# Expert layer of a two-block transformer: 224 tokens gather their rows, 288 meet every expert, value rows inside the planned order

## The chip, the cores and the metric

The kernel runs on one core of one Trainium2 chip. Its engines are PE (matmul; PEld is its weight load), DVE, ACT, POOL and SP, which here only issues DMAs. Sixteen DMA engines move data between DRAM and the on-chip buffer. The metric is device time in microseconds (us), the median of several executions.

## The reference, cut to what matters

The program is a whole network of two blocks on 512 tokens of width 1024. The change lies in its expert layer, the last step of the first block. The layer has 16,384 experts, each a row u and a row v of 1024 numbers. Each token has 8 heads; each head scores two sets of 128 keys, takes the best 16 of each, forms the 256 sums and keeps the best 16. So every token chooses 128 experts:

```python
def peer_ffn(xn, w_query, sub_keys, expert_u, expert_v):
    q = (xn @ w_query).reshape(bsz, seq, PEER_HEADS, 2, PEER_HALF)
    scores = jnp.einsum("bshpd,hpnd->bshpn", q, sub_keys)
    s_top, i_top = lax.top_k(scores, PEER_TOPK)
    ...
    best, pos = lax.top_k(cand, PEER_TOPK)
    idx = jnp.take_along_axis(cand_idx, pos, axis=-1)
    gates = jax.nn.softmax(best, axis=-1)
    ...
        u = expert_u[it]
        v = expert_v[it]
        act = gelu(jnp.einsum("td,ted->te", xt, u))
        return jnp.einsum("te,ted->td", gt * act, v)
```

## The kernel before

The layer is `peer()`. It treats the 512 tokens as four tiles of 128 and in two ways.

**Tokens 0 to 255 (tiles 0 and 1) gather.** `fetch` issues on POOL, for tile `tt` and choice `s`, one indirect DMA that brings to each of 128 partitions (one token each) that token's row of 4 KB: 128 gathers of 512 KB for each tile and each of the two tables `er` (U) and `ev` (V), 512 in all. The rows land in a ring of 8 places that lies in the tiles `xh` and `xl`. A U row is multiplied and summed with the token's vector on DVE (`product`, recorded at L1000, the line of the helper through which the planned part issues DVE work); a V row is scaled and added to `y` on DVE (L1336).

**Tokens 256 to 511 (tiles 2 and 3) meet all experts.** Experts are seen as 128 groups ("U rows" and "V rows" in what follows) of 128. `weights` (L1014) loads one group of 512 KB on SP into one of three tiles `wraw`, `whi`, `wlo` with several buffers each. `hidden` multiplies U row r with the 256 tokens: 8 matmuls of 128x256 (L1063, two instructions each); ACT takes the gelu (L1068) and writes it to DRAM as `ge_d`, except for the last `KEEP` rows, which stay on the chip. `spread` makes for each token a grid of 128 x 128 gates: DVE and ACT build one-hot factors (`sq`, `acc`), a "put" multiplies them (4 matmuls of 128 columns, L1252), ACT copies the result to `gs` (L1255), and after every fourth put SP writes 1 MB of it to `G` in DRAM. V rows need G and ge: DVE multiplies `a = ge * gt` (L1317), PE adds `a` times the V row into `yb` in PSUM (8 matmuls of 128x256, L1339).

**The order.** `first` writes the order of DVE, ACT, POOL and PE by hand with a planner that counts an estimated DVE time. A step is one U row; a step lasts by plan `ROW` = 4.5 us, or 5.3 where a put stands in it. Into each step the planner puts a piece of the selection (`select`, DVE) and row products, one after `PACE` = 2.6 us of planned time while selection lasts and 1.4 after it. POOL fetches up to `LEAD` = 6 rows ahead of the product. Tile 1's choices are selected last, so its rows can be fetched only when selection is over. `second` then opens new pools and goes through V rows 127 to 0: `a` six steps ahead, two gathered V rows for each step, the 8 matmuls. Its DVE order is the program's, the rest is a scheduler's. SP's order is a scheduler's throughout. After the last V row come 4 additions of `yb` to `h`, 16 transposes of `y`, 4 additions of those (L1351), and the next norm's sums.

Of the kernel before, what the change touches and what calls it, by code (L numbers as in the profile page):

```python
# [18 lines left out]
T = 512  # L19
D = 1024  # L20
# [116 lines left out]
NT = T // 2  # L137
RING = 8
LEAD = 6
KEEP = 20  # L140
PACE = (2.6, 1.4)
ROW = (4.5, 5.3)
GATE = 6
# [9 lines left out]
class Build:  # L153
# [810 lines left out]
    def peer(self):  # L964
        tc = self.tc
        with tc.tile_pool(name="pg", bufs=1) as pg:
            self.pg = pg
            self.G = self.dp.tile([16, 128, 16, 8, 16], F32, name="G")
            self.ge_d = [self.dp.tile([128, NT], F32, name=f"ge_d{j}") for j in range(128 - KEEP)]
# [7 lines left out]
            self.xb = pg.tile([128, 8, NT], F32, name="xb")  # L977
# [45 lines left out]
    def fetch(self, upto):  # L1023

        while self.nr < upto:
            table, n = divmod(self.nr, 256)
            tt, s = divmod(n, 128)
            self.nc.gpsimd.indirect_dma_start(  # L1028
                out=self.row(self.nr), out_offset=None,
                in_=self.A[("er", "ev")[table]].rearrange("j p a b -> (j p) (a b)"),  # L1030
                in_offset=bass.IndirectOffsetOnAxis(ap=self.ix[:, tt, s:s + 1], axis=0))
            self.nr += 1

    def product(self, pace):
# [22 lines left out]
    def hidden(self, r):  # L1057
# [4 lines left out]
        for k in range(8):  # L1062
            nc.tensor.matmul(ps[:, :NT], w[:, k], self.xb[:, k], start=k == 0, stop=k == 7)  # L1063

        def done():
            if r < 128 - KEEP:
                ge = self.pg.tile([128, NT], F32, name="ge", bufs=3)
                nc.scalar.activation(ge, ps[:, :NT], AF.Gelu)  # L1068
                nc.scalar.dma_start(self.ge_d[r], ge)
            else:  # L1070
                ge = self.ge[r] = self.pg.tile([128, NT], F32, name=f"ge{r}")
                nc.scalar.activation(ge, ps[:, :NT], AF.Gelu)
        self.later(1, done)

    def first(self, pt, pw, pps):
# [908 lines left out]
```

## Time and profile before

| | us |
|---|---|
| median of three executions (2762.29 to 2764.92) | 2762.43 |
| the profiled execution | 2763.71 |
| its span, first to last instruction | 2761.9 |
| expert layer, U rows begin to V rows end, about 618 to 1834 | 1216 |

The profile is one execution; times below are microseconds from the start of its span. A row that groups instructions gives their busy time, the mean of one in ns, and how long the engine had been idle just before them, with what ended that idleness. A row of a timeline gives start, length, engine, line, operation and operands, and in brackets the idle time before. Engine busy shares are averages over stages of different kinds, so stretches are read one by one.

### The profile page before, as it was taken

The numbers are of one execution on the slowest core, as the hardware profiler recorded it, in microseconds if no ns is written. First come the engines' busy times: TensorE is split into PE (matmuls) and PEld (weight loads), VectorE is DVE, ScalarE is ACT, GpSimd is POOL, SyncE is SP. The second block draws the span as 40 slices with busy tenths as digits, with TensorE's granted clock in tenths as the row PEclk, the third lists the DMA queues.
The fourth block names the chain that finished last, engine by engine and source line by source line (L and its number), as shares of the span: only waits on it lengthen the run. The fifth ranks groups of instructions, "written<-read, shape, count | busy, mean of one in ns | idle before, by whom it ended". The sixth has DMA issues, their size and how long they took to land.

```text
span 2761.9 us, 33459 instructions
## 1 busy us (share of the span) xinstructions
PE 2446.6 (89%) x11548; PEld 2020.4 (73%) x11548; DVE 1829.5 (66%) x3670; ACT 933.1 (34%) x1806; POOL 1318.7 (48%) x930
## 2 busy tenths in 40 slices
PE   7999998999889997784988888888999998999997
PEld 5778877878778886663866766776777786777776
DVE  6654353357999997657666666676697757666226
ACT  4432343331147775400000000022477734333323
POOL 5433357343333256646554445654324555455543
PEclk9999999999999999897999999999999999999998
DMA  5311123139999999999999999972202252222332
GB/s 193 100 61 31 47 75 125 49 126 340 330 311 339 333 344 410 407 410 407 407 405 405 405 405 405 402 267 66 81 24 74 94 161 81 92 84 92 105 115 86
DMA packets 227882, 600.26 MB, mean 217 GB/s; under 512 B 25601, under 2 KB 90753, under 8 KB 225281
## 3 DMA queue, kind: packets, MB, share of 16 engines
q1 hardware_dynamic: 126688, 298.75, 31.3%
q0 software_dynamic: 73728, 268.47, 25.1%
q10 hardware_dynamic: 27296, 30.90, 3.2%
q8 instruction: 92, 1.51, 0.2%
q14 instruction: 78, 0.63, 0.1%
HBM read 556.09 MB, written 41.94 MB: 217 GB/s over the span
## 4 chain that ended last, share of the span: by engine, by line
PE 31%; DVE 27%; DMA 23%; issue 8%; ACT 6%; POOL 4%; ACTq 0%; SPq 0%; DVEq 0%; POOLq 0%
PE mm L224 7%; PE mm L225 7%; PE mm L223 6%; DMA gl<-ge_d 6%; DVE y L1868 5%; DMA G<-gs 5%; DMA wraw<-in_ev_dram 3%; DMA xl<-in_ev_dram,ix 3%; PE mm L1063 3%; DMA whi<-in_ev_dram 2%; DVE xl L1000 2%; DVE xh L1000 2%; ACT whi L216 2%; PE dl L737 2%; DMA gt<-G 1%
## 5 line engine op out<-in xcount | busy, mean ns | idle before, releaser
L219 POOL TENSOR_TENSOR wlo<-wraw,whi 128x1024 fp32r<-128x1024 f32 (+5 forms) x212 | 466.2, 2205 | 467.0 <-ACT whi L216 461.1
L216 ACT ACTIVATE whi<-wraw 128x1024 fp32r<-128x1024 f32 (+4 forms) x213 | 204.2, 965 | 830.3 <-DMA wraw<-in_w_in_dram 567.4
L225 PE MATMUL mm<-xh,wlo 128*128 128x512 f32 (+1 forms) x1016 | 408.1, 402 | 20.5 <-POOL wlo L219 20.5
L224 PE MATMUL mm<-xl,whi 128*128 128x512 f32 (+1 forms) x1016 | 408.5, 403 | 3.3 <-DVE xl L338 2.3
L223 PE MATMUL mm<-xh,whi 128*128 128x512 f32 (+1 forms) x1016 | 404.9, 401 | 6.4 <-ACT xh L335 3.0
L225 PEld LDWEIGHTS mm<-xh,wlo 128*128 128x128 f32 (+1 forms) x1016 | 193.5, 190 | 68.8 <-POOL wlo L219 32.5
L1028 POOL DMA_INDIRECT xh<-in_ev_dram,ix x128 | 167.6, 1310 | 159.4 <-DVE y L1336 141.7
L1028 POOL DMA_INDIRECT xh<-in_er_dram,ix x128 | 145.1, 1133 | 194.3 <-DVE xh L1000 56.5
L1028 POOL DMA_INDIRECT xl<-in_er_dram,ix x128 | 148.9, 1163 | 172.1 <-DVE xl L1000 49.3
L1339 PE MATMUL yb<-a,wlo 128*128 128x256 f32 x688 | 169.4, 403 | 67.4 <-issue 40.7
L224 PEld LDWEIGHTS mm<-xl,whi 128*128 128x128 f32 (+1 forms) x1016 | 193.8, 191 | 45.9 <-DVE xl L338 6.1
L223 PEld LDWEIGHTS mm<-xh,whi 128*128 128x128 f32 (+1 forms) x1016 | 193.0, 190 | 46.3 <-ACT xh L335 3.9
L1336 DVE SCALAR_TENSOR_TENSOR y<-xl,gate,y 128x1024 f32<-128x1024 f32 x128 | 164.5, 1285 | 71.9 <-DMA xl<-in_ev_dram,ix 69.9
L1339 PEld LDWEIGHTS yb<-a,wlo 128*128 128x128 f32 x688 | 137.3, 203 | 96.2 <-issue 69.1
L1336 DVE SCALAR_TENSOR_TENSOR y<-xh,gate,y 128x1024 f32<-128x1024 f32 x126 | 163.5, 1298 | 41.5 <-DMA xh<-in_ev_dram,ix 40.3
L1868 DVE SCALAR_TENSOR_TENSOR y<-u,cvec,y 128x511 f32<-128x511 f32 (+1 forms) x88 | 137.0, 1560 | 74.6 <-ACT y L1866 73.2
L1339 PE MATMUL yb<-a,wraw 128*128 128x256 f32 x688 | 163.8, 393 | 21.7 <-DMA wraw<-in_ev_dram 20.7
L1028 POOL DMA_INDIRECT xl<-in_ev_dram,ix x128 | 132.8, 1037 | 104.5 <-DVE y L1336 81.2
L1000 DVE SCALAR_TENSOR_TENSOR xh<-xh,xt 128x1024 f32<-128x1024 f32 x128 | 155.8, 1217 | 38.1 <-DMA xh<-in_er_dram,ix 37.4
L1339 PE MATMUL yb<-a,whi 128*128 128x256 f32 x672 | 160.2, 393 | 22.5 <-DMA whi<-in_ev_dram 22.4
L1063 PE MATMUL mm<-xb,wlo 128*128 128x256 f32 x672 | 161.3, 396 | 16.7 <-DMA wlo<-in_eu_dram 9.9
L1000 DVE SCALAR_TENSOR_TENSOR xl<-xl,xt 128x1024 f32<-128x1024 f32 x128 | 155.9, 1218 | 28.3 <-DMA xl<-in_er_dram,ix 27.9
(654 smaller groups left out, 5108.7 us busy)
## 6 DMA issues: line engine op xcount, KB each, us to landing
wraw<-in_w_in_dram SPq DMA_DIRECT2D x57, 512.0 KB, 3.5
wraw<-in_w_up_dram SPq DMA_DIRECT2D x44, 512.0 KB, 3.5
wraw<-in_eu_dram SPq DMA_DIRECT2D x43, 512.0 KB, 6.6
whi<-in_eu_dram SPq DMA_DIRECT2D x43, 512.0 KB, 6.7
wlo<-in_ev_dram SPq DMA_DIRECT2D x43, 512.0 KB, 16.8
wraw<-in_ev_dram SPq DMA_DIRECT2D x43, 512.0 KB, 16.8
wlo<-in_eu_dram SPq DMA_DIRECT2D x42, 512.0 KB, 7.4
whi<-in_ev_dram SPq DMA_DIRECT2D x42, 512.0 KB, 16.8
```

Source lines behind the costliest of these rows:

```text
L216: nc.scalar.activation(hi, src, AF.Copy)
L219: (eng_lo or nc.vector).tensor_tensor(lo, src, hi.bitcast(F32), op=OP.subtract)
L223: t.matmul(ps, wh, xh, start=first, stop=False)
L224: t.matmul(ps, wh, xl, start=False, stop=False)
L225: t.matmul(ps, wl, xh, start=False, stop=last)
L737: te.matmul(ps[:, h * 128:(h + 1) * 128], lhs(h), rhs(h), start=True, stop=True)
L1000: return getattr(self.nc.vector, name)(out, *a, **kw)
L1028: self.nc.gpsimd.indirect_dma_start(out=self.row(self.nr), out_offset=None, in_=self.A[("er", "ev")[table]].rearrange("j p a b -> (j p) (a ...
L1063: nc.tensor.matmul(ps[:, :NT], w[:, k], self.xb[:, k], start=k == 0, stop=k == 7)
L1336: keep(v.scalar_tensor_tensor(y, r, a, y, op0=OP.mult, op1=OP.add))
L1339: te.matmul(yb[d // 2][:, d % 2], w[:, d], a, start=n == 0 and d % 2 == 0, stop=n == 127, skip_group_check=True)
L1868: v.scalar_tensor_tensor(y[:, j:], u[:, :T - j], w(2 - j), y[:, j:], op0=OP.mult, op1=OP.add)
```

## The change

`NT`, the number of tokens that gather, goes from 256 to 224. Tile 1 is split: its first 96 tokens gather, its last 32 join tiles 2 and 3, so that ND = 288 tokens meet all experts. Gathers of tile 1 bring rows to 96 partitions, and the products on them work on 96 partitions. U and V matmuls, gelus and gate products have 288 columns in place of 256, `ge_d` tiles are 128x288, and `G` has 18 blocks of 16 tokens in place of 16 (72 puts in place of 64). `KEEP` is 14 in place of 20. One-hot factors are made on ACT for the fourth part of every second block only, in place of every block.

`first` and `second` become one function, `experts`, with one planned loop of 256 steps: 128 U rows, then 128 V rows in the order 119 to 112, 127 to 120, 111 to 0. Four small functions serve the V steps: `ahead` (weights and ge, five steps ahead, in the U loop's last steps already), `gates` (eight rows of G at a time into one half of a tile that holds `q` until then), `gated` (the product of ge and gates, three steps ahead, into one of 7 slices of a `gs` buffer) and `value` (8 matmuls of 128x288 into 8 banks of PSUM that bear the names `sp`, `gp`, `mm`). The two sums `y` lie in the places of `kz` and `eq`. The planner goes on placing products of gathered V rows through all 256 steps. `ROW` becomes 4.4, 4.8 (with a put) and 3.7 (V step). After the loop come 8 additions of 128x288, 16 transposes, 4 additions of 128x2x224, and then the norm's sums.

```diff
-                self.first(pt, pw, pps)
+                self.experts(pt, pw, pps)
             self.np_open()
-            with tc.tile_pool(name="pv", bufs=2) as pv, \
-                    tc.tile_pool(name="pps", bufs=1, space=PSUM) as pps:
-                self.second(pv, pps)
+            for d in range(8):
+                self.stat2(d)
+                self.raw(d, self.gp[:, d:d + 1])
...
-NT = T // 2
+NT = 224
+ND = T - NT
+NB = ND // 16
+TOK = (128, NT - 128, 0, 0)
 RING = 8
 LEAD = 6
-KEEP = 20
+KEEP = 14
 PACE = (2.6, 1.4)
-ROW = (4.5, 5.3)
-GATE = 6
+ROW = (4.4, 4.8, 3.7)
+AOFF = 24
...
+            m = TOK[tt]
             self.nc.gpsimd.indirect_dma_start(
-                out=self.row(self.nr), out_offset=None,
+                out=self.row(self.nr)[:m], out_offset=None,
                 in_=self.A[("er", "ev")[table]].rearrange("j p a b -> (j p) (a b)"),
-                in_offset=bass.IndirectOffsetOnAxis(ap=self.ix[:, tt, s:s + 1], axis=0))
+                in_offset=bass.IndirectOffsetOnAxis(ap=self.ix[:m, tt, s:s + 1], axis=0))
...
+        table, n = divmod(n, 256)
         tt, s = divmod(n, 128)
-        r = self.row(n)
+        m = TOK[tt]
+        r = self.row(self.nf)[:m]
         self.nf += 1
-        self.dve("scalar_tensor_tensor", r, r, 1.0, self.xt[:, tt], op0=OP.mult, op1=OP.mult,
-                 accum_out=self.hid[:, tt, s:s + 1])
+        if table == 0:
+            self.dve("scalar_tensor_tensor", r, r, 1.0, self.xt[:m, tt], op0=OP.mult,
+                     op1=OP.mult, accum_out=self.hid[:m, tt, s:s + 1])
+        else:
+            a, y = self.gate[:m, tt, s:s + 1], self.y[tt][:m]
+            if s == 0:
+                self.dve("tensor_scalar", y, r, a, None, op0=OP.mult)
+            else:
+                self.dve("scalar_tensor_tensor", y, r, a, y, op0=OP.mult, op1=OP.add)
...
-            nc.tensor.matmul(ps[:, :NT], w[:, k], self.xb[:, k], start=k == 0, stop=k == 7)
+            nc.tensor.matmul(ps[:, :ND], w[:, k], self.xb[:, k], start=k == 0, stop=k == 7)
         def done():
             if r < 128 - KEEP:
-                ge = self.pg.tile([128, NT], F32, name="ge", bufs=3)
-                nc.scalar.activation(ge, ps[:, :NT], AF.Gelu)
+                ge = self.pg.tile([128, ND], F32, name="ge", bufs=5)
...
-                self.known = 128 * tt + (h0 + n) * K
+                self.known = 128 * tt + (h0 + n) * K if tt == 0 else 512
...
-            for tb in range(8):
+            for tb in range((128 - TOK[tt]) // 16):
...
-                        if t4 == 3:
+                        if t4 == 3 and tb % 2:
...
+        grids = (x for tt in (2, 3, 1) for x in spread(tt))
         load = lambda r: self.wts.update({r: self.weights(A["eu"][r])}) if r < 128 else None
+        yb, gt, vw, va = [], {}, {}, {}
+        order_v = [*range(119, 111, -1), *range(127, 119, -1), *range(111, -1, -1)]
+        def ahead(i):
+            if not 0 <= i < 128:
+                return
+            j = order_v[i]
+            vw[j] = self.weights(A["ev"][j])
+            if j < 128 - KEEP:
+                self.ge[j] = self.pg.tile([128, ND], F32, name="ge", bufs=5)
+                nc.sync.dma_start(self.ge[j], self.ge_d[j])
+        def gates(i):
+            if i % 8 or not 0 <= i < 128:
+                return
+            if not gt:
+                self.gt2 = pt.tile([128, 2, NB * 128], F32, name="q")
+                self.y = [pt.tile([128, D], F32, name="kz"), pw.tile([128, D], F32, name="eq")]
+                self.a = pw.tile([128, 2048], F32, name="gs", bufs=2)
+            gt[i // 8] = self.gt2[:, i // 8 % 2].rearrange("p (b j t) -> p b j t", j=8, t=16)
+            nc.sync.dma_start(gt[i // 8], self.G[order_v[i] // 8])
+        def gated(i):
+            if not 0 <= i < 128:
+                return
+            j = order_v[i]
+            c = AOFF + i % 7 * ND
+            va[j] = self.a[:, c:c + ND]
+            v("tensor_tensor", va[j].rearrange("p (b t) -> p b t", t=16),
+              self.ge.pop(j).rearrange("p (b t) -> p b t", t=16), gt[i // 8][:, :, j % 8],
+              op=OP.mult)
+        def value(i):
+            j = order_v[i]
+            if not yb:
+                yb.extend([pps.tile([128, T], F32, name="sp", bufs=2) for _ in range(2)] +
+                          [pps.tile([128, T], F32, name="gp", bufs=3) for _ in range(3)] +
+                          [self.pp.tile([128, T], F32, name="mm") for _ in range(3)])
+            a, w = va.pop(j), vw.pop(j)
+            for d in range(8):
+                te.matmul(yb[d][:, :ND], w[:, d], a, start=i == 0, stop=i == 127)
...
-            while self.step < 128 or work or grids or self.after or self.nf < 256:
+            while self.step < 256:
+                i = self.step - 128
                 self.due(False)
                 load(self.step + 5)
-                if self.step < 128:
+                ahead(i + 5)
+                gates(0 if i == -6 else i + 11 if i > -6 else -1)
+                gated(i + 3)
+                if i < 0:
                     self.hidden(self.step)
-                end += ROW[(self.step, True) in self.after]
+                    end += ROW[(self.step, True) in self.after]
+                else:
+                    value(i)
+                    end += ROW[2]
...
-                        self.spent = end if self.nf == 256 else min(end, self.when + PACE[1])
+                        self.spent = end if self.nf == 512 else min(end, self.when + PACE[1])
...
-    def second(self, pv, pps):
...
+                assert i != -7 or not grids
+            self.when = -99.0
+            while self.product(0.0):
+                self.when = -99.0
         self.xh, self.xl = (self.cp.tile([128, 8, T], F32R, name=n) for n in ("xh", "xl"))
-        for b in range(4):
+        for d in range(8):
+            h = self.h[:, d, NT:]
+            v("tensor_tensor", h, h, yb[d][:, :ND], op=OP.add)
+        for d in range(0, 8, 2):
             tp = self.pp.tile([128, T], F32, name="mm").rearrange("p (e t) -> p e t", e=2)
             for e in range(2):
                 for tt in range(2):
-                    d = 2 * b + e
-                    te.transpose(tp[:, e, tt * 128:(tt + 1) * 128],
-                                 self.y[:, tt, d * 128:(d + 1) * 128], self.ident)
-            for t, o in ((yb[b], NT), (tp, 0)):
-                h = self.h[:, 2 * b:2 * b + 2, o:o + NT]
-                nc.vector.tensor_tensor(h, h, t, op=OP.add)
-            for d in (2 * b, 2 * b + 1):
-                self.stat2(d)
-                self.raw(d, self.gp[:, d:d + 1])
+                    m = TOK[tt]
+                    te.transpose(tp[:, e, tt * 128:tt * 128 + m],
+                                 self.y[tt][:m, (d + e) * 128:(d + e + 1) * 128],
+                                 self.ident[:m, :m])
+            h = self.h[:, d:d + 2, :NT]
+            v("tensor_tensor", h, h, tp[:, :, :NT], op=OP.add)
```

**SP, where U rows end and V rows begin.** `eu` and `ev` are the U and V weights, `G` is the grid in DRAM, `gt` (before) and `q` (after) are its copies on the chip, `gl` is a ge that is read back; the numbers behind names count tiles. Before:

```order
L1014 DMA wraw_9139<-in_ev_dram 128x1024
L1014 DMA whi_9157<-in_ev_dram 128x1024
L1311 DMA gt_9095<-G_4299 128x2048
L1311 DMA gt_9153<-G_4299 128x2048
L1311 DMA gt_9283<-G_4299 128x2048
L1315 DMA gl_9349<-ge_d107_4407 128x256
L1315 DMA gl_9367<-ge_d106_4406 128x256
L1315 DMA gl_9385<-ge_d105_4405 128x256
L1315 DMA gl_9403<-ge_d104_4404 128x256
L1014 DMA wlo_9173<-in_ev_dram 128x1024
L1311 DMA gt_9421<-G_4299 128x2048
```

After, from the last write of the grid on:

```order
L1019 DMA wlo_8999<-in_eu_dram 128x1024
L1273 DMA G_4299<-gs_8780 128x16x128
L1019 DMA wraw_9018<-in_eu_dram 128x1024
L1307 DMA q_9039<-G_4299 128x2304
L1019 DMA whi_9037<-in_eu_dram 128x1024
L1307 DMA q_9039<-G_4299 128x2304
L1019 DMA wlo_9063<-in_ev_dram 128x1024
L1019 DMA wraw_9082<-in_ev_dram 128x1024
L1019 DMA whi_9101<-in_ev_dram 128x1024
```

Before, three readings of G stand behind the last U weight and nine V weights. Now the first reading stands among the last U weights, two rows behind the last write of G, and the V weights follow behind the readings.

**DVE, in the middle of the V rows.** `a` (before) and `gs` (after) receive ge times gates, `y` (before) and `kz` (after) are tile 0's sum, and `xh`, `xl` are the ring of gathered rows. Before:

```order
L1336 SCALAR_TENSOR_TENSOR y_9090<-xl_4697,gate_4411,y_9090 128x1024
L1317 TENSOR_TENSOR a_9643<-gl_9641,gt_9567 128x256
L1336 SCALAR_TENSOR_TENSOR y_9090<-xh_4696,gate_4411,y_9090 128x1024
L1336 SCALAR_TENSOR_TENSOR y_9090<-xl_4697,gate_4411,y_9090 128x1024
L1317 TENSOR_TENSOR a_9661<-gl_9659,gt_9567 128x256
```

After:

```order
L1005 TENSOR_TENSOR gs_9042<-ge_9835,q_9039 128x288
L1005 SCALAR_TENSOR_TENSOR kz_9040<-xh_4702,gate_4418,kz_9040 128x1024
L1005 SCALAR_TENSOR_TENSOR kz_9040<-xl_4703,gate_4418,kz_9040 128x1024
L1005 TENSOR_TENSOR gs_9042<-ge_9854,q_9039 128x288
L1005 SCALAR_TENSOR_TENSOR kz_9040<-xh_4702,gate_4418,kz_9040 128x1024
L1005 SCALAR_TENSOR_TENSOR kz_9040<-xl_4703,gate_4418,kz_9040 128x1024
L1005 SCALAR_TENSOR_TENSOR kz_9040<-xh_4702,gate_4418,kz_9040 128x1024
L1005 TENSOR_TENSOR gs_9042<-ge_9871,q_9039 128x288
```

Two row products stand between two gate products before; two or three do now.

**DVE, at the end of the layer.** `h` is the layer's result, `yb` (before) and `sp` (after) are matmul sums, `eq` is tile 1's sum. Before:

```order
L1336 SCALAR_TENSOR_TENSOR y_9090<-xl_4697,gate_4411,y_9090 128x1024
L1336 SCALAR_TENSOR_TENSOR y_9090<-xh_4696,gate_4411,y_9090 128x1024
L1336 SCALAR_TENSOR_TENSOR y_9090<-xl_4697,gate_4411,y_9090 128x1024
L1351 TENSOR_TENSOR h_69<-h_69,yb0_9091 128x2x256
L1351 TENSOR_TENSOR h_69<-h_69,yb1_9092 128x2x256
```

After:

```order
L1005 SCALAR_TENSOR_TENSOR eq_9041<-xh_4702,gate_4418,eq_9041 96x1024
L1005 SCALAR_TENSOR_TENSOR eq_9041<-xl_4703,gate_4418,eq_9041 96x1024
L1005 TENSOR_TENSOR gs_9042<-ge_11301,q_9039 128x288
L1005 TENSOR_TENSOR gs_9042<-ge_11317,q_9039 128x288
L1005 TENSOR_TENSOR gs_9042<-ge_11332,q_9039 128x288
L1005 TENSOR_TENSOR h_69<-h_69,sp_9163 128x288
L1005 TENSOR_TENSOR h_69<-h_69,sp_9164 128x288
```

The last gathered row stood right ahead of the additions; now three gate products stand between them, and so three V rows' matmuls come after the last gathered row.

## Rows read from the trace of the kernel before

**Rows 1.** The page: the span, and GB/s moved in each of its 40 equal slices.

```profile
span 2761.9 us, 33459 instructions
...
GB/s 193 100 61 31 47 75 125 49 126 340 330 311 339 333 344 410 407 410 407 407 405 405 405 405 405 402 267 66 81 24 74 94 161 81 92 84 92 105 115 86
```

**Rows 2.** Stretches: length, then busy PE, PEld, DVE, ACT, POOL, PEclk, DMA share, GB/s.

```profile
618.00:800.00 182.00, 160.35 (x716) 137.95 (x715) 160.82 (x515) 31.32 (x67) 66.81 (x61) 0.97 0.93 329
800.00:1011.00 211.00, 197.34 (x1052) 175.00 (x1051) 204.63 (x671) 157.06 (x370) 68.89 (x62) 0.98 0.97 333
1011.00:1240.00 229.00, 181.64 (x858) 155.85 (x856) 160.51 (x305) 93.32 (x228) 142.73 (x119) 0.92 1.03 402
1240.00:1280.00 40.00, 0.00 (x0) 0.00 (x0) 27.65 (x46) 0.58 (x2) 23.25 (x23) 0.56 1.03 411
1280.00:1834.00 554.00, 482.85 (x2048) 401.63 (x2049) 367.57 (x381) 1.06 (x1) 295.56 (x249) 0.94 1.03 403
```

**Rows 3.** DMA traffic from 618 to 1011, and its total and queues from 1280 to 1834.

```profile
DMA packets 62379, 130.10 MB, mean 331 GB/s; under 512 B 4794, under 2 KB 35898, under 8 KB 62347
...
DMA packets 70860, 223.42 MB, mean 403 GB/s; under 512 B 7883, under 2 KB 21707, under 8 KB 68965
## 3 DMA queue, kind: packets, MB, share of 16 engines
q0 software_dynamic: 35893, 130.67, 59.6%
q1 hardware_dynamic: 34938, 92.37, 42.7%
```

**Rows 4.** Groups by line, 600 to 1860: busy, mean ns, idle before.

```profile
L1339 PE MATMUL yb<-a,wlo 128*128 128x256 f32 x688 | 169.4, 403 | 67.4 <-issue 40.7 <-DMA wlo<-in_ev_dram 26.6
L1336 DVE SCALAR_TENSOR_TENSOR y<-xl,gate,y 128x1024 f32<-128x1024 f32 x128 | 164.5, 1285 | 71.9 <-DMA xl<-in_ev_dram,ix 69.9
...
L1317 DVE TENSOR_TENSOR a<-gl,gt 128x256 f32<-128x256 f32 x108 | 45.5, 422 | 71.2 <-DMA gl<-ge_d 71.2
```

**Rows 5.** L1063 alone, then L1252 alone: length, PE busy, PEld, PEclk, DMA share, GB/s.

```profile
618.00:800.00 182.00, 150.78 (x677) 130.85 (x676) 0.97 0.93 329
800.00:1011.00 211.00, 158.16 (x693) 130.13 (x692) 0.98 0.97 333
...
800.00:1011.00 211.00, 45.56 (x336) 44.17 (x336) 0.98 0.97 333
```

**Rows 6.** Timeline of PE: a U row of 16 instructions, a put, the next row.

```profile
847.80 3.62 PE L1063 MATMUL mm<-xb,whi 128*128 128x256 f32 x16
851.25 1.05 PE L1252 MATMUL gp<-acc,sq 128*128 128x128 f32 x8
852.14 1.03 PE L1063 MATMUL mm<-xb,wlo 128*128 128x256 f32 x4
```

**Rows 7.** DMA issues, 1011 to 1240 and 1280 to 1834: count, KB, median us to landing.

```profile
G<-gs SPq DMA_DIRECT2D x6, 1024.0 KB, 29.0
...
gt<-G SPq DMA_DIRECT2D x13, 1024.0 KB, 18.0
...
xh<-in_ev_dram,ix POOLq DMA_INDIRECT x124, 15.2
```

**Rows 8.** Stretches as in rows 2, while 64-partition loads of `kz` run.

```profile
573.00:573.50 0.50, 0.50 (x4) 0.41 (x3) 0.00 (x0) 0.00 (x0) 0.50 (x1) 1.00 1.05 312
```

**Rows 9.** Timeline: from U to V rows, and the end of the layer.

```profile
1279.78 2.44 DVE L1317 TENSOR_TENSOR a<-ge,gt 128x256 f32<-128x256 f32 x7 [7.52 <-DMA gt<-G]
...
1280.31 4.61 PE L1339 MATMUL yb<-a,wlo 128*128 128x256 f32 x10 [40.73 <-issue]
...
1830.69 3.62 PE L1339 MATMUL yb<-a,wraw 128*128 128x256 f32 x16
...
1838.64 2.47 DVE L1351 TENSOR_TENSOR h<-h,yb 128x512 f32<-128x512 f32 x4
...
1843.65 0.80 PE L223 MATMUL mm<-xh,whi 128*128 128x512 f32 x1 [0.77 <-ACT xh L335]
```

More of the change, by code (lines that the diff above doesn't have):

```diff
@@ L967, in peer @@
             self.pg = pg
-            self.G = self.dp.tile([16, 128, 16, 8, 16], F32, name="G")
-            self.ge_d = [self.dp.tile([128, NT], F32, name=f"ge_d{j}") for j in range(128 - KEEP)]
+            self.G = self.dp.tile([16, 128, NB, 8, 16], F32, name="G")
+            self.ge_d = [self.dp.tile([128, ND], F32, name=f"ge_d{j}") for j in range(128 - KEEP)]
             self.ge = {}
@@ L976, in peer @@
                 self.np_close()
-            self.xb = pg.tile([128, 8, NT], F32, name="xb")
+            self.xb = pg.tile([128, 8, ND], F32, name="xb")
+            self.xt = pg.tile([128, 2, D], F32, name="xt")
             self.ix = pg.tile([128, 2, 128], U32, name="ix")
@@ L1211, in select @@
             v("tensor_tensor", gt, gt, sm[:, :, None].to_broadcast([128, n, K]), op=OP.mult)
-            if tt >= 2:
+            if tt:
                 def turn():
@@ L1265, in first @@
         work = (x for o in order for x in select(*o))
-        grids = (x for tt in (2, 3) for x in spread(tt))
+        grids = (x for tt in (2, 3, 1) for x in spread(tt))
         load = lambda r: self.wts.update({r: self.weights(A["eu"][r])}) if r < 128 else None
+        yb, gt, vw, va = [], {}, {}, {}
[35 more added lines that the diff above has]
+                te.matmul(yb[d][:, :ND], w[:, d], a, start=i == 0, stop=i == 127)
         with self.tc.manual_schedule(engines=ENGINES):
@@ L1296, in first @@
                 self.step += 1
-    def second(self, pv, pps):
-        nc, A = self.nc, self.A
-        v, te = nc.vector, nc.tensor
-        keep = self.tc.keep_in_program_order
-        gt = {}
-        self.y = pv.tile([128, 2, D], F32, name="y", bufs=1)
-        def gated(j):
-            g8 = j // 8
-            if g8 not in gt:
-                gt.clear()
-                gt[g8] = pv.tile([128, 16, 8, 16], F32, name="gt", bufs=3)
-                nc.sync.dma_start(gt[g8], self.G[g8])
-            ge = self.ge.get(j)
-            if ge is None:
-                ge = pv.tile([128, NT], F32, name="gl", bufs=6)
-                nc.sync.dma_start(ge, self.ge_d[j])
-            a = pv.tile([128, NT], F32, name="a", bufs=GATE + 2)
-            keep(v.tensor_tensor(a.rearrange("p (b t) -> p b t", t=16),
-                                 ge.rearrange("p (b t) -> p b t", t=16), gt[g8][:, :, j % 8],
-                                 op=OP.mult))
-            return a, self.weights(A["ev"][j])
-        yb = [pps.tile([128, 2, NT], F32, name=f"yb{b}") for b in range(4)]
-        rows = list(range(127, -1, -1))
-        nxt = [gated(j) for j in rows[:GATE]]
-        for n in range(128):
-            if n + GATE < 128:
-                nxt.append(gated(rows[n + GATE]))
-            for m in (2 * n, 2 * n + 1):
-                tt, sl = divmod(m, 128)
-                self.fetch(256 + m + 1)
-                r = self.row(256 + m)
-                a, y = self.gate[:, tt, sl:sl + 1], self.y[:, tt]
-                if sl == 0:
-                    keep(v.tensor_scalar(y, r, a, None, op0=OP.mult))
-                else:
-                    keep(v.scalar_tensor_tensor(y, r, a, y, op0=OP.mult, op1=OP.add))
-            a, w = nxt.pop(0)
-            for d in range(8):
-                te.matmul(yb[d // 2][:, d % 2], w[:, d], a, start=n == 0 and d % 2 == 0,
-                          stop=n == 127, skip_group_check=True)
@@ L1341, in second @@
+                assert i != -7 or not grids
+            self.when = -99.0
+            while self.product(0.0):
+                self.when = -99.0
+            assert not self.after
         self.xh, self.xl = (self.cp.tile([128, 8, T], F32R, name=n) for n in ("xh", "xl"))
-        for b in range(4):
+        for d in range(8):
+            h = self.h[:, d, NT:]
+            v("tensor_tensor", h, h, yb[d][:, :ND], op=OP.add)
+        for d in range(0, 8, 2):
             tp = self.pp.tile([128, T], F32, name="mm").rearrange("p (e t) -> p e t", e=2)
```

36 lines of the change are left out of this document (19 added, 17 removed).

## Prediction, made before the changed kernel ran

> **What bounds the kernel now.** I read the page's slices first: from about 618 to 1834 us the core moves 311 to 411 GB/s, far more than before or after [rows 1]. That is the expert layer. Then I cut it into stretches [rows 2], since the bound changes inside it. From 618 to 1011 selection runs: DMA moves 329 to 333 GB/s, while DVE is busy 161 of 182 us and then 205 of 211, PE 160 and 197. Here the planned order and DVE are the limit and DMA has room. From 1011 to 1834 DMA moves 402 to 411 GB/s in every stretch, with a busy share of 1.03, and PE and DVE have room: in the V rows PE is busy 483 of 554 us and DVE 368. What they wait for there is data: the sums wait 70 us for gathered rows, the gate products 71 us for ge, PE 27 us for one of three weight tiles [rows 4]. Even the 40 us in which PE does nothing between U and V rows [rows 2, 9] run at 411 GB/s, so they cost DMA nothing. So the layer's length is the bytes over about 403 GB/s, plus the room that DMA leaves unused before 1011, plus the tail behind the last transfer.
>
> **Bytes.** Of the V rows' 223 MB, the gathers' queue moves 131 and the weights' and grids' queue 92 [rows 3]. U and V weights are loaded as before. The change takes 32 of 128 rows of 4 KB out of 256 gathers (tile 1, both tables): 256 x 32 x 4096 B = 33.55 MB less. It adds: ge was written and read for 108 rows of 131 KB and will be for 114 of 147 KB, 2.65 MB more each way; the grid has 18 MB-sized blocks of tokens in place of 16, 2.10 MB more each way. Together 33.55 - 5.30 - 4.20 = 24.05 MB less. At 0.403 MB/us [rows 2] that is **-59.7 us**, if a gather of 96 rows costs 96/128 of a full one.
>
> **The first stretch, to the end of selection.** Before, it has 677/16 = 42.3 U rows in 182 us and 693/16 = 43.3 rows in 211 us [rows 5]: 4.30 and 4.87 us for each. A U row of 256 columns takes 851.25 - 847.80 = 3.45 us of PE and a put 852.14 - 851.25 = 0.89 [rows 6]; 288 columns make 3.45 x 288/256 = 3.88. By the plan of the changed kernel selection ends in step 92, and puts begin in step 41.
> Steps 0 to 40: the plan gives 4.4 in place of 4.5 us, so DVE's side becomes 4.30 x 4.4/4.5 = 4.21. PE needs 3.88 and, for scores and the rest, (160.35 - 150.78)/42.3 = 0.23, which is 4.11 [rows 2, 5]. DVE leads; 41 x 4.21 = 173 us.
> Steps 41 to 91, each with a put: DVE had 204.63/43.3 = 4.73 us of work in a step, and 4.8/5.3 of that is 4.28. PE needs 3.88 + 0.89 and some 0.15 for the 23 other instructions (1052 - 693 - 336) [rows 2, 5]: 4.92. Here PE takes over the bound; 51 x 4.92 = 251 us.
> Together 424 us, against 393. By then the changed kernel has moved the 130.1 MB of before [rows 3] and 3.4 for 6.4 more weights, 2.7 for ge and 2.1 for two more writes of the grid, 138.3 MB; the gathers are the same, since tile 1's can't start earlier. Room left unused: 393 x 0.403 - 130.1 = 28.3 MB before, 424 x 0.403 - 138.3 = 32.6 after. The difference of 4.3 MB costs **+10.6 us**. If PE can't run without gaps (it was busy 197 of 211 us beside a busy DVE), 0.1 us in each of 51 steps makes 5 more; the low end is nothing.
>
> **Do PE and DVE keep up behind that?** In the V steps remain 283 gathers (128 MB), 123 weights (64.5), ge (16.8) and G (18.9): 228 MB or 566 us, 4.42 us for each step. PE needs 3.88, DVE 283 x 1.29 us for sums and 128 x 0.45 for gate products [rows 4], 3.3 for each step. DMA stays the bound there, with 12% to spare on PE instead of the 20% of before (3.45 of 4.33 us). The widened work on ACT has no place on this path: ACT does nothing in the V rows [rows 2]. A product on 96 partitions I take to last as long as one on 128, 1.29 us; were it shorter, nothing would change, as DVE waits anyway.
>
> **From U to V rows.** The pause of PE goes, but it cost DMA nothing, so I book no gain. A new wait can come: the first gate product stands in DVE's order three steps ahead of the first V row, with row products queued behind it, and these release the ring for POOL's gathers. It waits for G, which waits for the grid's last write. That write landed 29.0 us after issue and a reading takes 18.0 [rows 7], 47 us, and the order gives it some eight steps of 4.8, 38 us. So DVE may stand still for up to 9 us or so; of the ring's eight rows up to six are in flight then, and weights standing behind the reading on SP go on. Before, DVE waited 7.5 us for G there [rows 9] at full DMA. Bounds: 0, and 12 us with all of it lost. I take **+5 us**, between them, because DMA is lost only when ring and weights both run dry.
>
> **The tail.** Before, the last V row's matmuls start at 1830.69, DVE's last sums end and the additions begin at 1838.64, and the next stage's first matmul starts at 1843.65 [rows 9]: some 8 us from the last landed rows to that matmul. After, three gate products stand behind the last sum, so three V rows, 3 x 3.88 = 11.6 us, then eight additions (2.47/4 us for 512 columns, so 0.35 for 288, 2.8 in all), one of the other four, 0.6, and the 2 to 3 us that the norm takes: 18 us. That is **+10 us**. Bounds: +4, if PE has run ahead of the sums, and +22, if PE is three more V rows behind when the last row lands.
>
> **The sum.** -59.7 + 10.6 + 5 + 10 = -34 us. The profiled execution took 2763.7 us, 1.3 above the median; 2763.7 - 34 - 1.3 = **2728 us**. Its own range: all three costs at their low ends, -59.7 + 0 + 0 + 4 = -56, gives 2707; at their high ends, -59.7 + 15.6 + 12 + 22 = -10, gives 2752.
>
> **Rival 1, ending slower: a narrow gather takes as long as a full one.** If the time of a gather is set by its deepest part and not by its bytes, each of the 256 gathers of tile 1 keeps its 0.524/0.403 = 1.30 us in place of 0.98. Then the 33.55 MB are saved on paper alone, 83 us come back, and the time is 2728 + 83 = 2811. It decides from 0.98 + 34/256 = 1.11 us for a gather upward: there the gain is gone. No gather of 96 rows is in the trace. The nearest row is a load to 64 partitions: for half a microsecond it moves 312 GB/s, with the DMA engines' share at 1.05, thus all sixteen at work [rows 8]. That is above half of 403, which a load tied to half of the paths would have had, and speaks against the rival, over a short window and with one other kind of transfer. Chance 0.15.
> [...]
>
> **Rival 2: DMA is not kept full.** The plan spreads the gathers over 256 steps. Where a V step is rich in rows or DVE waits in order for a row, the gate product behind it is late, PE is late, and weights are asked for late. With six rows of 15.2 us each in flight [rows 7] the queue can bring 0.39 rows/us at that landing time; the V steps need 283/566 = 0.50, so the landing has to become shorter, as it must have been in 1011 to 1240: 119 gathers in 229 us, 0.52 in each, at 402 GB/s [rows 2]. That speaks against a shortfall. For one: PE's clock was 0.94 in the V rows [rows 2], and its spare time falls from 20 to 12%. At 97% of the rate over the 744 us from 1042 on, 22 us are lost: 2750; at 95%, 37 us: 2765. Chance 0.20, around 2750.
>
> **Rival 3: more comes free.** If the tail hides behind the norm's first sums and PE's puts fill gaps that DVE leaves, only the bytes count: 2763.7 - 59.7 - 1.3 = 2703, or a little less. Chance 0.08.
>
> **How the numbers follow.** The forecast has 0.57, the rivals 0.15, 0.20 and 0.08. A measurement of this kernel can tell about 0.2% from no change, 5.5 us, so "same" is 2757 to 2768. The forecast and rival 3 lie below, about 0.63 with a hundredth or two lost to "same"; of rival 2, 0.12 lies below, 0.05 within, 0.03 above; rival 1 lies above, in part within, since a gather may cost something between. Faster 0.75, same 0.08, slower 0.17. The range reaches from rival 3's 2700 to 2775, which takes in rival 2 and a gather at about 1.15 us and leaves out rival 1's full price.
>
> **What the changed profile would show.** Selection should end near 1042, with PE busy nearly throughout from step 41. From there to the last V row DMA should stand at 400 GB/s or more, with about 24 MB less moved in the layer. The gathers of tile 1 should land faster than those of tile 0. If GB/s falls to some 330 wherever tile 1's rows run while the DMA share stays at 1.0, rival 1 holds; if GB/s and share fall together, rival 2. A gap on PE and DVE near step 125 longer than 12 us would break the term of the U to V step, and more than 25 us from the last gathered row to the next stage's first matmul the tail's.

## The result: 2941 us, 6.4% slower

The changed kernel takes 2940.94 us (median of four, 2938.25 to 2944.89) against 2763.68 for the kernel before; the ratio is 1.064, interval 1.062 to 1.066. The forecast was 2728, faster by 1.3%. The profiled execution took 2941.22 us; its span is 2939.4.

The page of the changed kernel, DMA and GB/s in 40 slices of the span, answers to [rows 1]:

```profile
span 2939.4 us, 33700 instructions
...
DMA  5311131279999999999999999994211252222332
GB/s 189 101 51 37 46 116 58 84 254 340 326 319 306 337 311 310 284 293 321 405 406 406 298 270 266 264 258 124 72 55 37 76 165 87 91 92 86 103 103 95
```

The stage after selection no longer runs at one rate. There is a middle part of some 260 us at 405 GB/s, and a part before and a part behind it at 260 to 320. The DMA digits stay at 9 all through: the engines are as busy as ever and move less.

The stretches (length, busy PE, PEld, DVE, ACT, POOL, granted clock, DMA share, GB/s) show it better, to be held against [rows 2]:

```profile
618.00:800.00 182.00, 176.78 (x721) 136.80 (x719) 158.33 (x508) 30.16 (x62) 66.12 (x61) 0.99 0.93 331
800.00:1042.00 242.00, 238.64 (x1184) 196.35 (x1185) 219.32 (x720) 167.76 (x387) 65.13 (x63) 0.99 0.94 320
1042.00:1260.00 218.00, 167.97 (x751) 133.56 (x749) 137.77 (x279) 91.25 (x210) 117.22 (x98) 0.89 1.03 299
1260.00:1380.00 120.00, 94.51 (x340) 69.81 (x341) 65.25 (x113) 1.13 (x3) 44.46 (x47) 0.91 1.02 296
1380.00:1640.00 260.00, 214.85 (x815) 155.19 (x814) 173.89 (x173) 0.00 (x0) 122.94 (x122) 0.97 1.03 404
1640.00:1990.00 350.00, 248.93 (x836) 177.67 (x836) 184.09 (x183) 0.00 (x0) 128.00 (x124) 0.88 1.03 263
1990.00:2018.00 28.00, 25.36 (x110) 19.69 (x108) 10.15 (x19) 4.43 (x6) 7.11 (x4) 0.97 0.43 136
```

The fast stretch, 1380 to 1640, is the one in which tile 0's V rows land, with 128 rows in a gather: POOL issues them from 1358 to 1629. Before that it issues tile 1's U rows (1057 to 1357), after it tile 1's V rows (1631 to 1975), with 96 rows in a gather. A share of 1.03 goes with 404 GB/s in the one case and with 263 in the other.

The DMA traffic of 1380 to 1640, then of 1640 to 1990, by queue, with the issues of gathers into `xh` (count and median us from issue to landing); q0 carries the gathers, q1 the weights, ge and G:

```profile
DMA packets 33106, 104.99 MB, mean 404 GB/s; under 512 B 3686, under 2 KB 10337, under 8 KB 32324
q0 software_dynamic: 17672, 64.33, 62.8%
q1 hardware_dynamic: 15420, 40.48, 40.0%
...
xh<-in_ev_dram,ix POOLq DMA_INDIRECT x61, 15.3
...
DMA packets 30153, 92.21 MB, mean 263 GB/s; under 512 B 3794, under 2 KB 10519, under 8 KB 29373
q0 software_dynamic: 14257, 50.07, 56.6%
q1 hardware_dynamic: 15884, 41.99, 46.3%
...
xh<-in_ev_dram,ix POOLq DMA_INDIRECT x62, 18.5
```

Engine time for one MB is share x 16 engines x length / MB. On q0 it is 0.628 x 16 x 260 / 64.33 = 40.6 us with full gathers and 0.566 x 16 x 350 / 50.07 = 63.3 with narrow ones. On q1 it is 41.1 and 61.7: the weights, which are loaded to 128 partitions as ever, become dearer by half too, and one of their tiles, `whi`, lands 22.3 us after issue in place of 10.4. So a narrow gather does not only take longer itself; what is under way beside it slows down.

### The profile page after: what moved, and what is told of

The parts are those of the page before. It is cut to its first block, busy times and chain, and to the rows that moved or that the text cites. A ratio compares the mean times of both kernels' runs of the same rounds, so it can differ in the third digit from the quotient of the medians.

```text
span 2939.4 us, 33700 instructions
## 1 busy us (share of the span) xinstructions
PE 2588.3 (88%) x11615; PEld 2036.7 (69%) x11615; DVE 1849.5 (63%) x3734; ACT 941.7 (32%) x1801; POOL 1266.9 (43%) x930
## 3 DMA queue, kind: packets, MB, share of 16 engines
q10 hardware_dynamic: 28160, 33.55, 3.3%
## 4 chain that ended last, share of the span: by engine, by line
PE 36%; DMA 28%; DVE 20%; issue 6%; ACT 6%; POOL 4%; ACTq 0%; DVEq 0%; SPq 0%; POOLq 0%
DMA xl<-in_ev_dram,ix 9%; PE mm L1078 8%; PE mm L229 6%; PE mm L228 6%; PE mm L227 6%; DVE y L1898 5%; DMA xh<-in_ev_dram,ix 4%; DMA ge<-ge_d 4%; DMA xl<-in_er_dram,ix 3%; DMA G<-gs 3%; ACT whi L220 2%; PE gp L1267 2%; PE dl L741 2%; POOL wlo L223 1%; DVE xl L1005 1%
## 5 line engine op out<-in xcount | busy, mean ns | idle before, releaser
L220 ACT ACTIVATE whi<-wraw 128x1024 fp32r<-128x1024 f32 (+4 forms) x213 | 204.3, 965 | 906.6 <-DMA wraw<-in_w_in_dram 634.5
L227 PE MATMUL mm<-xh,whi 128*128 128x512 f32 (+1 forms) x1016 | 404.2, 401 | 10.4 <-ACT xh L339 6.7
L1034 POOL DMA_INDIRECT xh<-in_ev_dram,ix x128 | 132.2, 1033 | 180.4 <-DVE eq L1005 93.9
L1078 PE MATMUL mm<-xb,wraw 128*128 128x288 f32 x688 | 181.4, 419 | 21.8 <-DMA wraw<-in_eu_dram 21.8
L1005 DVE SCALAR_TENSOR_TENSOR xh<-xh,xt 128x1024 f32<-128x1024 f32 (+1 forms) x128 | 155.6, 1216 | 46.8 <-DMA xh<-in_er_dram,ix 46.6
L1078 PE MATMUL mm<-xb,wlo 128*128 128x288 f32 x672 | 176.4, 417 | 2.1 <-DMA wlo<-in_eu_dram 2.1
L1005 DVE SCALAR_TENSOR_TENSOR xl<-xl,xt 128x1024 f32<-128x1024 f32 (+1 forms) x128 | 156.0, 1218 | 35.2 <-DMA xl<-in_er_dram,ix 35.1
L1078 PEld LDWEIGHTS mm<-xb,wraw 128*128 128x128 f32 x688 | 133.6, 197 | 58.5 <-issue 22.6
L1078 PE MATMUL mm<-xb,whi 128*128 128x288 f32 x688 | 173.9, 406 | 0.0
L1078 PEld LDWEIGHTS mm<-xb,wlo 128*128 128x128 f32 x672 | 129.9, 196 | 37.4 <-issue 2.6
L1078 PEld LDWEIGHTS mm<-xb,whi 128*128 128x128 f32 x688 | 129.1, 190 | 33.6
L1005 DVE SCALAR_TENSOR_TENSOR eq<-xl,gate,eq 96x1024 f32<-96x1024 f32 x64 | 81.9, 1280 | 53.2 <-DMA xl<-in_ev_dram,ix 52.8
```

The source lines that it names most:

```text
L220: nc.scalar.activation(hi, src, AF.Copy)
L227: t.matmul(ps, wh, xh, start=first, stop=False)
L1005: return getattr(self.nc.vector, name)(out, *a, **kw)
L1034: self.nc.gpsimd.indirect_dma_start(out=self.row(self.nr)[:m], out_offset=None, in_=self.A[("er", "ev")[table]].rearrange("j p a b -> (j p ...
L1078: nc.tensor.matmul(ps[:, :ND], w[:, k], self.xb[:, k], start=k == 0, stop=k == 7)
```

## The experiments

A price is used below: what one of tile 1's 256 gathers costs in DMA time. A full gather costs 0.5243 MB / 0.405 = 1.295 us, 1.30 for short. By its bytes alone a gather of 96 rows would cost 0.97. The price of a narrow one is 1.295 plus the difference in time to the same kernel with full gathers, over 256. So it holds what the gather does to the transfers beside it as well.

**Full gathers in the changed kernel.** The gathers bring 128 rows; nothing else changes.

```diff
-            m = TOK[tt]
+            m = 128
             self.nc.gpsimd.indirect_dma_start(
```

> The changed kernel, but tile 1's gathers bring all 128 rows; the 32 rows more are never used. Theory A (a gather of 96 rows into 96 partitions slows every transfer beside it): from 1680 to 1960 us of the changed kernel DMA moves some 265 GB/s at a share of 1.04, 74 MB, of which about 104 gathers of 0.393 MB; the other 33 MB at 405 GB/s need 82 us, so a narrow gather costs about 1.9 us there, some 1.8 on average over the 256, against 1.30 for a full one. Without narrow gathers DMA goes back to 400 to 405 GB/s in all full stretches and the time is 2941 - 256 x 0.5 = 2813, within 20 us. Theory B (the new order of rows, weights, ge and G on the queues is at fault, not the width): 33.55 MB more are moved at the same poor rate, and the time rises by 83 us or more, to 3024 or above.

Measured: 2817.7 us (ratio 1.018, interval 1.016 to 1.020). 33.55 MB more, and 123 us less. Its V rows before and after 1640, in the columns of the stretches above:

```profile
1245.00:1640.00 395.00, 339.39 (x1262) 247.93 (x1262) 262.21 (x307) 0.31 (x1) 194.76 (x186) 0.94 1.03 406
1640.00:1860.00 220.00, 184.96 (x688) 133.87 (x687) 146.06 (x146) 0.00 (x0) 104.90 (x104) 0.95 1.03 405
```

Theory A holds, theory B falls. The average price of a 96-row gather is 1.295 + (2940.9 - 2817.7)/256 = 1.78 us.

**Narrow gathers in the kernel before.** Only the width of tile 1's gathers changes, with the products on the same 96 partitions; the old order stays, and the last 32 tokens of tile 1 get no expert output.

```diff
+GW = (128, 96)
...
-                out=self.row(self.nr), out_offset=None,
+                out=self.row(self.nr)[:m], out_offset=None,
```

> The kernel before with one thing changed: tile 1's gathers bring only the first 96 rows; its last 32 tokens get no expert output (left out). The order and everything else stay. Theory A: each of the 256 narrow gathers costs about 0.5 us more than a full one although it moves a quarter less, +128 us, so about 2890, with GB/s falling to some 265 to 310 at a DMA share of 1.03 or more wherever tile 1's rows run. Theory B: 33.55 MB less at 0.403 MB/us, 83 us less, about 2680.

Measured: 2895.6 us (ratio 1.046, interval 1.044 to 1.048), where the bytes would have given 2680. Price: 1.295 + (2895.6 - 2765.8)/256 = 1.80 us, nearly the same as in the other order. Its V rows with tile 0's gathers, then with tile 1's:

```profile
1320.00:1560.00 240.00, 213.16 (x925) 179.50 (x924) 162.53 (x172) 0.00 (x0) 117.58 (x111) 0.96 1.03 405
1640.00:1900.00 260.00, 177.45 (x698) 143.91 (x699) 124.78 (x130) 0.00 (x0) 113.77 (x88) 0.88 1.04 265
```

The width alone takes the rate from 405 to 265, with no other part of the change present. Together the two runs show where the time went.

**The changed order without narrow gathers.** `NT = 256`; 256 tokens meet all experts and every gather is full.

```diff
-NT = 224
+NT = 256
```

> The changed kernel with NT = 256: no narrow gathers, 256 tokens meet all experts, but the one planned loop, the order of V rows, KEEP = 14 and the plan's steps are the changed kernel's. Theory A: only the small terms are left, tail +10, U to V step +5, KEEP +4, a first stretch that moves some 7 us worth of bytes more: within 20 us of the kernel before, about 2774. Theory B: the order is at fault, so most of the 177 us stay: 2880 or more.

Measured: 2787.7 us (ratio 1.0076, interval 1.0059 to 1.0093), 22 us over the kernel before where 10 were expected. So the new order is no gain in itself, but it is not what cost 177 us. Part of its excess is the tail:

```profile
1841.63 1.28 DVE L1005 SCALAR_TENSOR_TENSOR eq<-xl,gate,eq 128x1024 f32<-128x1024 f32 x1
...
1859.77 0.85 DVE L1005 TENSOR_TENSOR h<-h,sp 128x256 f32<-128x256 f32 x2 [13.88 <-PE sp L1327]
...
1865.85 0.97 PE L227 MATMUL mm<-xh,whi 128*128 128x512 f32 x3 [1.23 <-ACT xh L339]
```

From the end of the last row's product, 1842.9, to the next stage's first matmul pass 23 us, DVE waiting 13.9 of them for PE's V rows. Counted in the same way, 5 us passed in the kernel before, from 1838.64 to 1843.65 [rows 9]; the prediction's 8 count from the last landed rows.

**64 rows.** Tile 1's gathers cut to 64 rows; 32 more tokens get no expert output.

```diff
+GW = (128, 64)
...
-            m = TOK[tt]
+            m = GW[tt]
             self.nc.gpsimd.indirect_dma_start(
```

> The changed kernel with tile 1's gathers cut to 64 rows; the rows of 32 more tokens are left out, and these tokens get no expert output. Theory A1 (rows crowd into a part of the partitions, and the 64 lower ones are the crowded part): a gather of 64 rows costs hardly less than one of 96 or 128, GB/s falls below 265 at a DMA share above 1, and the time is between 2810 and 2941. [...]

Measured: 2862.2 us (one time). Price: 1.295 + (2862.2 - 2817.7)/256 = 1.47 us for half the bytes of a full gather. Its V rows with tile 0's gathers, then tile 1's:

```profile
1400.00:1560.00 160.00, 128.54 (x496) 93.09 (x496) 106.47 (x106) 0.00 (x0) 74.33 (x75) 0.99 1.03 405
1620.00:1860.00 240.00, 182.88 (x639) 134.15 (x638) 144.36 (x144) 0.00 (x0) 120.45 (x101) 0.87 1.02 243
```

So it isn't 96 rows alone that are dear: by its bytes a gather of 64 rows would cost 1.295/2 = 0.65 us. A1, crowding in the lower partitions, was still possible and went to the next run.

**The same 96 rows, every second gather 32 partitions higher.** Over two gathers the lower and the upper 64 partitions then get 96 rows each.

```diff
+    def place(self, tt, s):
+        return SHIFT * (s % 2) if tt else 0
...
-                out=self.row(self.nr)[:m], out_offset=None,
+                out=self.row(self.nr)[lo:lo + m], out_offset=None,
```

> The changed kernel with the same 96 rows in each of tile 1's gathers, but every second gather lands 32 partitions higher (32 to 127 in place of 0 to 95); products, a third sum y and a shifted copy of the gates follow it, KEEP is 10 to make room. Width, bytes and count of the narrow gathers stay. Theory P (what costs is that all narrow gathers fill the lower partitions: 64 of 96 rows go to the lower half, so the paths into that half stay behind): over two gathers both halves now get 96 rows, DMA goes back to some 400 GB/s and the time to that of the wide gathers less the bytes, 2818 - 83 + 3 for four more ge rows = 2738, within 25 us. [...]

Measured: 2935.0 us (ratio 1.061, interval 1.058 to 1.064). Theory P falls; the V rows with narrow gathers stay slow:

```profile
1440.00:1640.00 200.00, 165.98 (x629) 120.86 (x628) 133.49 (x133) 0.00 (x0) 92.90 (x95) 0.97 1.03 404
1680.00:1940.00 260.00, 185.62 (x617) 132.44 (x616) 138.13 (x138) 0.00 (x0) 95.33 (x96) 0.88 1.04 269
```

What is lost does not depend on filling one half more than the other, summed over gathers: 269 GB/s here, 263 in the changed kernel. What is left is something within a single transfer, perhaps how its rows are dealt out (theory Q in what follows); this run doesn't show what.

**112 rows.** 16 of them are never used.

```diff
-            m = TOK[tt]
+            m = (128, 112)[tt]
             self.nc.gpsimd.indirect_dma_start(
```

> The changed kernel with tile 1's gathers of 112 rows, 16 of them never used. A gather of 128 rows costs 1.30 us of DMA (run with wide gathers), one of 96 rows 1.90, one of 64 rows 1.62 (each from a stretch of V rows: length less the other bytes at 405 GB/s, over the count). [...] Rival (cost falls to the full one as the width nears 128): about 1.3 to 1.5, 2818 to 2860.

Measured: 2975.3 us (one time), so a price of 1.295 + (2975.3 - 2817.7)/256 = 1.91 us. Its V rows with tile 1's gathers:

```profile
1740.00:1990.00 250.00, 174.10 (x576) 123.85 (x575) 122.38 (x122) 0.00 (x0) 78.81 (x85) 0.87 1.04 273
```

The cost does not fall towards the full width; it rises with the bytes until, at 128 rows, it drops by a third: 1.47, 1.78, 1.91 and 1.30 us for 64, 96, 112 and 128 rows.

**Narrow loads on another queue.** In the kernel before, each U and V weight load is split in two; all gathers are full.

```diff
-        self.nc.sync.dma_start(t, src)
+        self.nc.sync.dma_start(t[:96], src[:96])
+        self.nc.sync.dma_start(t[96:], src[96:])
```

> The kernel before with each of the 256 U and V weight loads on SP split in two, partitions 0 to 95 and 96 to 127. Same bytes, all gathers full. It asks whether the cost of a narrow transfer is one of the gathers on POOL's queue or of any transfer of fewer than 128 partitions. Theory Q for every queue: a load of 96 rows costs about 0.9 us of DMA more than its bytes as a narrow gather does (1.90 against 0.97), 256 x 0.9 = 230 us, and the 32-row loads, two rows for each engine, cost more than theirs; the time is 2950 or more, GB/s near 270 in the V rows. Rival (gathers alone): the same 2764, within 15 us, at 400 GB/s or more from 1011 on; between them, a part of it.

Measured: 3073.1 us (one time), 306 us above the kernel before, with the same bytes. Two stretches of its V rows:

```profile
1400.00:1700.00 300.00, 220.45 (x827) 176.24 (x825) 142.18 (x146) 0.00 (x0) 108.69 (x98) 0.87 1.04 297
1700.00:2000.00 300.00, 194.54 (x719) 154.80 (x720) 130.26 (x136) 0.00 (x0) 124.13 (x90) 0.86 1.04 273
```

So it is neither the gather nor POOL's queue: plain loads of SP to 96 and to 32 partitions do the same, at the same share of 1.04. The split leaves open which of the two widths costs how much. By queue, the second stretch reads:

```profile
q0 software_dynamic: 12815, 46.66, 58.5%
q1 hardware_dynamic: 14513, 35.00, 45.1%
```

Now the gathers are full and the loads narrow, and the gathers suffer: 0.585 x 16 x 300 / 46.66 = 60.2 us of engine time for one MB, against 40.6 beside full loads. The larger number of loads alone is not the reason. The kernel before issues 450 transfers in the 500 us from 1300 to 1800, 102 of them reads of ge of only 128 KB, and moves 405 GB/s; 1.2 us of DMA time for each transfer as such would come to 540 us.

**Rows spread to the end of the plan.** Full gathers, and a V step planned at 3.6 us.

```diff
-ROW = (4.4, 4.8, 3.7)
+ROW = (4.4, 4.8, 3.6)
```

> The changed kernel with wide gathers in tile 1, and a V step planned at 3.6 us in place of 3.7, so that the plan places the last row's product in step 253 of 256 in place of 249. In the run with wide gathers 18 us pass from the last row's product (1876.4) to the next stage's first matmul (1894.6), during which DMA is nearly idle. Theory: the rest of that is PE's work on V rows behind the last gathered row; with the rows spread to the end some two to three V rows of 3.9 us go, 2818 - 10 = 2808, within 5 us. Rival: the last V row is set by its own weights and ge, which are then asked for later; 2815 to 2820, no gain.

Measured: 2822.3 us, no gain on 2817.7. The rival has the result right but not the reason. The V rows do end earlier, and the additions with them; then the norm waits:

```profile
1876.86 1.28 DVE L1005 SCALAR_TENSOR_TENSOR eq<-xl,gate,eq 96x1024 f32<-96x1024 f32 x1
...
1880.23 3.58 DVE L1005 TENSOR_TENSOR h<-h,mm 128x288 f32<-128x288 f32 x7
...
1893.05 0.79 ACT L220 ACTIVATE whi<-wraw 128x704 fp32r<-128x704 f32 x1 [6.65 <-DMA wraw<-in_w_kg_dram]
1893.74 0.61 ACT L304 ACTIVATE acc<-h 128x512 f32<-128x512 f32 x1
```

The sums are done at 1883.8, but the norm's first operation stands in ACT's order behind a conversion of the next stage's weights (L220), which waits for their load. Ten microseconds pass there. In the run with wide gathers that wait lay under the V rows' end.

**Full gathers without waste.** Tile 1's 96 x 128 choices dealt over all 128 partitions: 96 gathers of 128 rows for each table. Partition 96+i takes the last 32 choices of tokens 3i, 3i+1 and 3i+2.

```diff
+PACKED = 96
+ROWS = 128 + PACKED
...
+    def pack(self, t):
+        for k in range(3):
+            self.nc.gpsimd.dma_start(t[96:, 1, 32 * k:32 * k + 32], t[k:96:3, 1, 96:])
...
-            m = TOK[tt]
+            m = 128
...
-            a, y = self.gate[:m, tt, s:s + 1], self.y[tt][:m]
+            a, y = self.gate[:m, tt, s:s + 1], self.y[tt + k]
...
+                for k in range(3):
+                    te.matmul(tp[:, e, 128:NT], self.y[1 + k][:, c], self.back[:, k],
+                              start=k == 0, stop=k == 2)
```

> The changed kernel with tile 1's 96 x 128 choices dealt out over all 128 partitions: partitions 96 to 127 take the last 32 choices of three tokens each, so each table needs 96 gathers of 128 rows in place of 128 gathers of 96 rows. Same bytes, 64 gathers and 64 products fewer. Small copies move indices, gates and token vectors to those partitions; three sums y are put together at the end by matmuls; KEEP is 6 to make room; PACE is 1.7 after selection, so that fewer products last to the end. Theory Q (a gather of fewer than 128 rows costs by how its rows are dealt out): all gathers are full, DMA stays at 400 to 405 GB/s behind selection, and the time is that of the wide gathers less 64 x 1.295 us, 2818 - 83, plus 6 for eight more ge rows, plus some 10 for the first indices' copy: 2750, between 2735 and 2765. Rival (fewer bytes don't help here, as PE's wider work sets the pace): DMA falls below 390 GB/s behind selection with its share below 1.0, and the time stays between 2790 and 2820.

Measured: 2749.0 us (2744.5 to 2749.5; ratio 0.9938, interval 0.9921 to 0.9955), faster than both kernels. Its V rows:

```profile
1245.00:1500.00 255.00, 234.10 (x902) 170.69 (x901) 167.66 (x195) 0.28 (x1) 128.82 (x119) 0.98 1.03 405
1500.00:1780.00 280.00, 248.91 (x956) 181.51 (x955) 174.33 (x182) 0.00 (x0) 158.32 (x120) 0.98 1.03 406
```

The gathers bring the same rows as the change's do, in fewer gathers dealt over all partitions; `KEEP`, `PACE` and the copies differ besides, as the expectation says. All V rows run at 405 GB/s, and against the run with wide gathers the saved bytes are paid out: 2749 where the sum gave 2750.

## Why the prediction was wrong

**The step that failed is the price of a narrow gather.** The part on bytes booked -59.7 us "if a gather of 96 rows costs 96/128 of a full one", that is 0.98 us. It costs 1.78 to 1.80. The 256 gathers, which were to save 83 us against full ones, cost 123 us more than full ones: 207 us between the forecast and the chip. 2728 + 207 = 2935, and 2941 was measured.

**The rival had the right sign and too small a size.** Rival 1 said that a narrow gather takes as long as a full one, 2811. I let the full gather be the upper bound of the unknown cost, with no row that excluded more, and then set the range's end below even that. The runs show a third state that neither bound held: the transfer is dearer than the wider one that contains it, 1.78 us against 1.30, and slows the rest of the traffic, 61.7 us for one MB on q1 against 41.1.

**The row that I held against it didn't bear it.** [rows 8] showed 312 GB/s in half a microsecond of a 64-partition load, in a stretch without other DMA work. That is the best half microsecond. From 570.5 to 575 the two loads of `kz`, one to each half of the partitions, are the only traffic:

```profile
DMA packets 1056, 0.52 MB, mean 117 GB/s; under 512 B 32, under 2 KB 1056, under 8 KB 1056
...
q10 hardware_dynamic: 1056, 0.52, 41.0%
```

That is 0.41 x 16 x 4.5 / 0.52 = 57 us of engine time for one MB, where full transfers take 41 (40.6 and 41.1 in 1380 to 1640 of the changed kernel). So the row itself already spoke for a dearer transfer, though its packets are also smaller, all under 2 KB, and no run parts the two. In a steady stream of 64-row gathers among other loads the rate is 243 GB/s at a share of 1.02.

**The other terms held, to 7 us in all.** The run with wide gathers tests them, since by the prediction's sum it should take 2811; it took 2817.7.
- Selection was to end near 1042 with PE as the bound: PE is busy 238.6 of 242 us in the changed kernel and 240.6 of 245 with wide gathers; in both, selection's last indices free tile 1's rows at 1041.6 and the last product on its gates stands at 1045.7.
- DMA was to stay full behind it: 405 to 406 GB/s in the V rows. Rival 2 did not happen there.
- The wait at the start of the V rows was put at 5 us, at most 12. It is 3.6 us for DVE with wide gathers. With narrow ones it is 17.5, more than the 12 that were to break this term. The transfers themselves are not what makes the difference: from the issue of the grid's last write to that of its reading pass 37.7 us, against 35.2 with wide gathers, and from there to the gate product 5.3 against 8.8. But the write stands behind weights and ge in SP's order, and is issued at 1222.2 there, 30.7 us later than with wide gathers (1191.5), while DVE comes to its gate product only 16 us later (1247.7 and 1231.9):

```profile
1265.23 0.46 DVE L1005 TENSOR_TENSOR gs<-ge,q 128x288 f32<-128x288 f32 x1 [17.54 <-DMA q<-G]
```

- The tail was put at 18 us from the last row. With wide gathers it is 1876.5 to 1894.6:

```profile
1875.24 1.28 DVE L1005 SCALAR_TENSOR_TENSOR eq<-xl,gate,eq 96x1024 f32<-96x1024 f32 x1 [1.25 <-DMA xl<-in_ev_dram,ix]
...
1885.49 0.94 DVE L1005 TENSOR_TENSOR h<-h,sp 128x288 f32<-128x288 f32 x2 [7.87 <-PE sp L1327]
...
1894.59 1.65 PE L227 MATMUL mm<-xh,whi 128*128 128x512 f32 x3 [4.03 <-ACT xh L339]
```

In the changed kernel itself it is 24 us (1994.4 to 2018.3). The expectation for `NT = 256` was less good, 10 us against 22. The tail there is 23 us in place of 18, and the first stretch, booked as 7 us gained, gains nothing: by 1030, where selection ends, 136.95 MB are moved in 412 us, which leaves 412 x 0.403 - 136.95 = 29.1 MB of room unused, against 28.3 in the kernel before.

**The test that the prediction set itself decided.** GB/s down with the DMA share still at 1.0, wherever tile 1's rows run, was to mean rival 1; GB/s and share down together, rival 2. The share is 1.03 at 263 GB/s. The gathers of tile 1, which were to land faster than tile 0's, land slower, after 18.5 us against 15.3.

**What stays open** is why a narrow transfer is dearer. The runs exclude the gather as such (the split loads cost it too, 1.2 us for each), the lower half of the partitions being filled more over several gathers (staggered 2935 us, not staggered 2941), and a count of rows that 16 doesn't divide (64, 96 and 112 are all multiples of 16, and cost 1.47, 1.78 and 1.91 us). That one half gets more rows than the other within a single transfer was not tested by itself; but a full gather brings the same 64 rows to the fuller half, so by this alone 96 rows would cost no more than 1.30. The cause within a transfer was not shown: no profile here shows which engine writes which partition.

## What to carry to other kernels

When a stage is bound by DMA, bytes saved by filling fewer than 128 partitions can be worse than no saving (2941 us here, 2818 with full gathers): look at GB/s beside the DMA share, and if the rate falls while the share stays at 1.0, each byte costs more engine time than before (here 263 GB/s in place of 404 at 1.03, and 63.3 us for one MB of gathers in place of 40.6). Deal the same rows over all 128 partitions instead, even at the price of small copies and an extra sum at the end (2749 us here). And where the trace has no row for a price, don't take "as dear as the larger case" for its upper bound; one short run that changes the width alone would have shown it.

## What the runs showed of the hardware

- Among full-width traffic, a gather of 4 KB rows costs 1.47, 1.78, 1.91 and 1.30 us of DMA time for 64, 96, 112 and 128 rows (2862.2, 2940.9, 2975.3 and 2817.7 us for the kernel), what it costs the transfers beside it included.
- SP's transfers to 128 partitions take 61.7 us of engine time for one MB beside narrow gathers, in place of 41.1; full gathers take 60.2 beside narrow loads, in place of 40.6.
- Loads of 128 rows split into 96 and 32 on SP's queue cost 306 us over 256 loads, 1.2 us for each (3073.1 us against 2767.0).
- A product on 96 partitions lasts as long as one on 128: 1.280 and 1.285 us in the V rows of the changed kernel.
- PE's granted clock was on average 0.88 with narrow V gathers (1640 to 1990 of the changed kernel) and 0.97 with full ones (1380 to 1640). PE was then busy 249 of 350 and 215 of 260 us. It waited 73 us for V weights in the first stretch and 44 us for gate products in the second, and DMA was full in both, at a share of 1.03; from this I take the clock to be no cause of the length here.
